# A one-core transformer block: one input loaded and split earlier, value products by unit, attention's matmuls moved between the rounded and the low blocks, turns of rows moved to later steps

## The chip, the cores and the metric

One core of a Trainium2 chip runs the whole kernel. The metric is the device time of one execution in microseconds (us). Engines: PE (TensorE) multiplies matrices, DVE (VectorE) and ACT (ScalarE) work on elements, POOL (GpSimd) does a few small things, SP (SyncE) issues most transfers; ACT's queue issues some too.

## The reference

One encoder layer on 256 tokens of width 2048, float32. Cut to what matters:

```
h = rms_norm(x, attn_norm);  proj = h @ w_in
qa, ka, va, qb, kb, vb, ga, gb = split(proj)
ya = windowed_gqa(qa, ka, va, table, sink)          # 8 heads, 2 key heads, |i-j| <= 128
yb = dilated_attention(qb, kb, vb, table)           # 3 groups of 4 heads, strides 1, 4, 16, merged per position
merged = sigmoid(ga) * (ya @ w_branch_a) + sigmoid(gb) * (yb @ w_branch_b)
x = x + merged @ w_out
hf = rms_norm(x, ffn_norm)
g = depthwise_conv3(hf @ w_ffn_gate)
x = x + (gelu(g) * (hf @ w_ffn_up)) @ w_ffn_down    # width 5632
x = x + sigmoid(rms_norm(x, ple_norm) @ w_ple_gate) * (p @ w_ple_proj)   # p: 256 x 256
return rms_norm(x, final_norm)
```

## The kernel before

Every weight is read once, in 263 pieces, mostly of 1 MB, that SP's queue loads into a ring of three buffers `raw` (L243). A piece is cut into units. For each unit ACT writes a rounded copy (L263, `uh` or `vh`) and DVE the remainder (L264, `ul` or `vl`), so that a float32 product is made of three products of the rounded type: rounded x rounded, rounded x low, low x rounded. Units of plain pieces live in a ring of six (`u`), those of Strassen pieces that need sums of weight blocks in a ring of two (`v`); the sums are three instructions on DVE, L256 to L258, ahead of the split. A unit is produced when the one that it replaces in its ring is dropped after its last matmul.

Stages, in order: A (the projections of queries, keys and values, with the attention heads in between), B0 to B3 with ba/bb (gates and branch products), D0 and D1 (output projection), E0 and E1 (gate and up), F00, F01, F10, F11 (down product, half of the inputs by half of the outputs each), pp0 and pp1 (p times `w_ple_proj`), G0, G2, G3 (the per-layer gate), then the final rows.

In A and E a job is one output block of 128 columns. It takes two units of eight blocks each (`unit_blocks`): sixteen matmuls of 128x512 with the rounded weights (L305; the 512 columns are the tokens' rounded and low halves), then sixteen of 128x256 with the low weights (L309). The value jobs are different (`value_product`): for each of sixteen blocks k, three matmuls into each of two banks (L343 to L345).

B, D, F, G0 and pp go by `quad_stage`: a piece of kind "S" is a Strassen step of 21 matmuls, one of kind "s" has 24 (L355 to L357). All are 128x512.

Small work hangs on steps. `at((stage, i, g), f)` registers f, and `run_due` calls it when the stage's loop arrives there. A head's scores are registered one job on at k = 9, the transposition of its softmax (`turn`, L666) in the job after that at k = 11 or 12, and its values (L612 to L614, and L681 for the far heads) another job on at k = 4. `turn` also copies the transposed rows to `near` on ACT and DVE, which the values need. `residual` adds the sums of D and F to the residual rows `xr` (L915, L917, and the square for the norm in L919), and `rows_pair` turns two blocks of 256 columns of these rows back (`turn_back`: four transpositions into one bank, L849, then two ACT L452 and two DVE L453 that write `pl`, the input of G). A bank such as P22 is one of eight in which matmuls add up; the sums M2, M3, M4, P22 of a stage keep theirs from their first matmul until L915 has read them.

The calls only give a dependence order and a program order as written; a scheduler then orders the instructions of each engine by its own cost estimates, except where `keep` fixes it.

The input p (`pair`, 256 KB) is needed in pp0 and pp1. Its rounded part is `ph_` (tiles `t`, L1001), its low part `pl_` (tiles `u`, L1002).

Of the kernel before, what the change touches and what calls it, by code (L numbers as in the profile page):

```python
# [187 lines left out]
def _encoder(ctx: ExitStack, tc, xt, pt, xrow, cols, gainrow, table, onehot, mask, ident_in, wts, out):  # L188
# [108 lines left out]
    def unit_blocks(todo):  # L297

        ends, units = [], []
        for _ in range(JOINED):  # L300
            u = _FBLOCKS[state["at"] + len(ends)][0]
            units.append(u)
            for o in range(_LAST_OF[u] + 1):
                acc, m, first, last = next(todo)
                nc.tensor.matmul(acc, weights(u)[0][:, o * P:(o + 1) * P], m,  # L305
                                 start=first, stop=False, skip_group_check=True)
                ends.append((acc, m, last, u, o))
        for acc, m, last, u, o in ends:
# [4 lines left out]
        state["at"] += len(ends)  # L313

    def products(i, moving, n, accs):

        def todo():
            for k in range(n):
                run_due(i, k)
                for acc in accs:  # L320
                    yield acc, moving(k), k == 0, k == n - 1

        blocks, end = todo(), state["at"] + n * len(accs)
        while state["at"] < end:
            unit_blocks(blocks)
# [7 lines left out]
    def value_product(i, paired, n):  # L333

        accs = [bank("acc") for _ in range(2)]
        for k in range(KC):
            run_due(i, k)
            u, o = _FBLOCKS[state["at"]]
            hi, lo = (w[:, o * P:(o + n) * P] for w in weights(u))
            for t, acc in enumerate(accs):  # L340
                tokens = (TWINS if paired else HALVES)[t]
                xh, xl = (hs[:, k, c:c + T][:, tokens] for c in (0, T))
                nc.tensor.matmul(acc[:, :n * P], xh, hi, start=(k == 0), stop=False)  # L343
                nc.tensor.matmul(acc[:, :n * P], xh, lo, start=False, stop=False)  # L344
                nc.tensor.matmul(acc[:, :n * P], xl, hi, start=False, stop=(k == KC - 1))  # L345
            state["at"] += n
            if o + n - 1 == _LAST_OF[u]:
                drop(u)
# [631 lines left out]

    for half in range(2):
# [14 lines left out]
        if half:  # L996
            pr = held["tok"].tile([P, 2, T], F32, name="pair", bufs=2)
            nc.scalar.dma_start(pr, pt)
            ph_, pl_ = ([sc.tile([P, T], FR, name=name) for _ in range(2)] for name in ("t", "u"))
            for k in range(2):  # L1000
                nc.scalar.activation(ph_[k], pr[:, k], AF.Copy)  # L1001
                nc.vector.tensor_tensor(pl_[k], pr[:, k], ph_[k].bitcast(F32), op=ALU.subtract)  # L1002
            held["ssq"] = sc.tile([P, 2, 2], F32, name="ssq", bufs=1)
        residual("F%d0" % half, 0, activation_row, "act", half)
        if half:
            pl = big.tile([P, KC, 2 * T], FR, name="pl", tag="R0")
            for pair, when in enumerate((("F11", 0, 2), ("F11", 0, 5), ("F11", 1, 0), ("F11", 1, 3))):
# [64 lines left out]
    for t in range(2):  # L1072
# [13 lines left out]
        for n in range(4):  # L1086
            row = xr[:, t, cut[n]]
            if n % 2:
# [58 lines left out]
```

## Time and profile before

| | |
|---|---|
| median of 3 runs | 1463.11 us (1462.89 to 1464.44) |
| profiled execution | 1462.99 us, of which the span of the profile is 1461.2 |
| PE | busy 1446.7 us, 7488 matmuls |
| DVE | busy 1248.4 us, 1839 instructions |
| ACT | busy 824.8 us, 1151 instructions |
| PE's granted clock | 0.998 of full speed |
| transferred | 282.88 MB, mean 194 GB/s |

The span is the time from the first to the last record on the core; the rest of the execution lies around it. A matmul's duration in the profile overlaps that of the next one, so the time between two starts is what a matmul takes of the run.

### The profile page before, as it was taken

Reading aid. Unit: us, or ns where it says so; the run is one execution under the profiler, and the core shown is the slowest. Engines: PE = TensorE matmul, PEld = TensorE weight load, DVE = VectorE, ACT = ScalarE, POOL = GpSimd, SP = SyncE. Lnnn points to the kernel's source line nnn. Section 1 sums busy time; section 2 is a strip of 40 time slices with the busy share of each in tenths; the row PEclk is TensorE's granted clock in tenths of the full one; section 3 lists DMA queues with packets and bytes.
Section 4 is the critical chain, followed back from the end, with each engine's and each line's share of the span. In section 5 each row is a group of like instructions: output and inputs, shape, how many; then the busy total and the mean of one; then the engine's idle time right before and its main releaser. Section 6 shows DMA issues by size and latency. Waiting matters only on the chain.

```text
span 1461.2 us, 19529 instructions
## 1 busy us (share of the span) xinstructions
PE 1446.7 (99%) x7488; PEld 1235.3 (85%) x7488; DVE 1248.4 (85%) x1839; ACT 824.8 (56%) x1151; POOL 4.9 (0%) x9
## 2 busy tenths in 40 slices
PE   9999999999999999999999999999999999999997
PEld 8888888888888888788888888888888888788785
DVE  7777664679998989989888899989888888999994
ACT  7555544456555655655555556555555555555763
POOL 0000000000000000000000000000000000000000
PEclk9999999999999999999999999999999999999999
DMA  9753444435546456465555545565455554546462
GB/s 323 259 206 144 169 160 166 174 138 202 199 187 238 180 205 233 170 247 185 192 184 193 183 172 200 200 232 202 181 194 185 190 189 164 192 183 235 168 231 86
DMA packets 46456, 282.88 MB, mean 194 GB/s; under 512 B 5076, under 2 KB 9812, under 8 KB 14108
## 3 DMA queue, kind: packets, MB, share of 16 engines
q1 hardware_dynamic: 45356, 280.20, 52.3%
q10 hardware_dynamic: 1008, 1.45, 0.3%
q8 instruction: 58, 0.95, 0.2%
q14 instruction: 34, 0.28, 0.1%
HBM read 279.49 MB, written 2.14 MB: 193 GB/s over the span
## 4 chain that ended last, share of the span: by engine, by line
PE 94%; DVE 2%; DMA 1%; ACT 1%; issue 1%; POOLq 0%; POOL 0%; ACTq 0%
PE bank L305 29%; PE bank L309 15%; PE bank L356 13%; PE bank L355 13%; PE bank L357 13%; PE bank L343 2%; PE bank L345 2%; PE bank L344 2%; PE bank L291 2%; PE bank L292 1%; DVE ul L264 1%; PE bank L849 1%; PE bank L666 0%; DMA pair<-in_pt 0%; DMA raw<-in_wts 0%
## 5 line engine op out<-in xcount | busy, mean ns | idle before, releaser
L263 ACT ACTIVATE uh<-raw 128x1024 fp32r<-128x1024 f32 (+2 forms) x518 | 521.8, 1017 | 397.9 <-PE bank L305 190.3
L264 DVE TENSOR_TENSOR ul<-raw,uh 128x1024 fp32r<-128x1024 f32 (+2 forms) x518 | 595.8, 1168 | 152.6 <-ACT uh L263 72.0
L305 PE MATMUL bank<-hf,uh 128*128 128x512 f32 x1408 | 336.5, 391 | 0.0
L305 PEld LDWEIGHTS bank<-hf,uh 128*128 128x128 f32 x1408 | 258.6, 188 | 50.1
L309 PEld LDWEIGHTS bank<-hf,ul 128*128 128x128 f32 x1408 | 180.6, 191 | 6.9
L309 PE MATMUL bank<-hf,ul 128*128 128x256 f32 x1408 | 183.0, 283 | 0.0
L263 ACT ACTIVATE vh<-raw 128x1024 fp32r<-128x1024 f32 x92 | 97.5, 1059 | 66.9 <-DVE raw L256 36.7
L264 DVE TENSOR_TENSOR vl<-raw,vh 128x1024 fp32r<-128x1024 f32 x92 | 111.8, 1217 | 0.4
L305 PE MATMUL bank<-hs,uh 128*128 128x512 f32 x432 | 109.2, 395 | 0.0
L355 PE MATMUL bank<-uh,act 128*128 128x512 f32 x232 | 90.4, 390 | 0.0
L357 PE MATMUL bank<-uh,act 128*128 128x512 f32 x232 | 90.4, 390 | 0.0
L356 PE MATMUL bank<-ul,act 128*128 128x512 f32 x232 | 90.4, 390 | 0.0
L305 PEld LDWEIGHTS bank<-hs,uh 128*128 128x128 f32 x432 | 77.7, 189 | 13.8
L436 ACT ACTIVATE t<-bank 128x256 f32<-128x256 f32 x122 | 46.4, 383 | 75.5 <-PE bank L309 70.1
L355 PE MATMUL bank<-uh,hs 128*128 128x512 f32 x172 | 67.3, 391 | 0.0
L357 PE MATMUL bank<-uh,hs 128*128 128x512 f32 x172 | 67.2, 391 | 0.0
L356 PE MATMUL bank<-ul,hs 128*128 128x512 f32 x172 | 67.1, 390 | 0.0
L309 PEld LDWEIGHTS bank<-hs,ul 128*128 128x128 f32 x432 | 55.4, 191 | 2.2
L256 DVE TENSOR_TENSOR raw<-raw 128x1024 f32<-128x1024 f32 x46 | 56.1, 1219 | 0.6
L356 PE MATMUL bank<-vl,S 128*128 128x512 f32 x138 | 54.4, 394 | 1.8 <-DVE vl L264 1.7
L309 PE MATMUL bank<-hs,ul 128*128 128x256 f32 x432 | 56.0, 282 | 0.0
L355 PE MATMUL bank<-vh,S 128*128 128x512 f32 x138 | 54.5, 399 | 0.3 <-ACT vh L263 0.3
(240 smaller groups left out, 2272.3 us busy)
## 6 DMA issues: line engine op xcount, KB each, us to landing
raw<-in_wts SPq DMA_DIRECT2D x251, 1024.0 KB, 4.8
raw<-in_wts SPq DMA_DIRECT2D x12, 512.0 KB, 6.7
xr<-in_xrow SPq DMA_DIRECT2D x4, 512.0 KB, 8.3
x<-in_xt SPq DMA_DIRECT2D x13, 128.0 KB, 5.7
hb<-hold SPq DMA_DIRECT2D x3, 514.0 KB, 5.9
hb<-hold SPq DMA_DIRECT2D x2, 768.0 KB, 7.1
last<-in_gainrow SPq DMA_DIRECT2D x1, 1024.0 KB, 5.0
out<-xr SPq DMA_DIRECT2D x4, 256.0 KB, 2.6
```

The lines of the kernel that those rows point to most:

```text
L256: nc.vector.tensor_tensor(raw[:, :2 * WIDE], raw[:, WIDE:3 * WIDE], raw[:, :2 * WIDE], op=ALU.subtract)
L263: nc.scalar.activation(hi, src, AF.Copy)
L264: nc.vector.tensor_tensor(lo, src, hi.bitcast(F32), op=ALU.subtract)
L291: nc.tensor.matmul(acc, hi[:, w], m, start=first, stop=False, skip_group_check=True)
L305: nc.tensor.matmul(acc, weights(u)[0][:, o * P:(o + 1) * P], m, start=first, stop=False, skip_group_check=True)
L309: nc.tensor.matmul(acc[:, T:], weights(u)[1][:, o * P:(o + 1) * P], m[:, :T], start=False, stop=last, skip_group_check=True)
L343: nc.tensor.matmul(acc[:, :n * P], xh, hi, start=(k == 0), stop=False)
L344: nc.tensor.matmul(acc[:, :n * P], xh, lo, start=False, stop=False)
L355: nc.tensor.matmul(acc, sh, wh, start=first, stop=False)
L356: nc.tensor.matmul(acc, sh, wl, start=False, stop=False)
L357: nc.tensor.matmul(acc, sl, wh, start=False, stop=last)
L436: keep(nc.scalar.activation(t, acc[:, T:], AF.Copy, scale=scale))
```

## The change

Five parts:
- `value_product` goes by unit: all blocks of a unit into the first bank, then all into the second (before: block by block, into both banks). What is due at k is run ahead of the first bank's matmuls of k.
- `unit_blocks` runs what is due at k up to 10 (scores, values) after the sixteen rounded matmuls and ahead of the sixteen low ones, and what is due at 11 to 13 (the transpositions) after the low ones. What is due at the first k of the two units still comes first. Before, all of it stood among the rounded matmuls.
- p is loaded by SP's queue at step (F10, 2, 0) and split at (F10, 9, 0). Before, it was loaded by ACT's queue and split in front of F10.
- In F11, the four turns of rows are registered at the steps (0, 6), (1, 2), (1, 5), (2, 1) instead of (0, 2), (0, 5), (1, 0), (1, 3).
- Of the final rows' four column blocks, DVE scales three and ACT one, instead of two each.

Line numbers move: L305 is L307 after, L309 L314, L343 to L345 L353 to L355, L355 to L357 L364 to L366, L447 and L448 L456 and L457, L612 to L614 L621 to L623, L666 L675, L681 L690, L849 L858, L974 and L975 L983 and L984, L1001 and L1002 L1000 and L1001.

PE's order in stage A, around one far head's values (`bank_1930` is the job's sum; `near` and `far` are the head's transposed rows). Before:

```order
L305 MATMUL bank_1930<-hs_102,uh_1766 128x512 x4
L612 MATMUL bank_1935<-near_1879,v_1109 128x256
L613 MATMUL bank_1935<-near_1879,v_1109 128x256
L614 MATMUL bank_1935<-near_1879,v_1109 128x256
L612 MATMUL bank_1935<-near_1879,v_1109 128x256
L613 MATMUL bank_1935<-near_1879,v_1109 128x256
L614 MATMUL bank_1935<-near_1879,v_1109 128x256
L681 MATMUL bank_1935<-far_1880,vf_1567 128x128 x4
L305 MATMUL bank_1930<-hs_102,uh_1766 128x512 x4
L305 MATMUL bank_1930<-hs_102,uh_1778 128x512 x8
L309 MATMUL bank_1930<-hs_102,ul_1767 128x256 x8
L309 MATMUL bank_1930<-hs_102,ul_1779 128x256 x8
```

The same job after, with the transpositions that end the job ahead of it:

```order
L675 MATMUL bank_1911<-ident_76,s_1805 128x128 x4
L675 MATMUL bank_1918<-ident_76,s_1805 128x128 x4
L307 MATMUL bank_1930<-hs_102,uh_1766 128x512 x8
L307 MATMUL bank_1930<-hs_102,uh_1778 128x512 x8
L621 MATMUL bank_1947<-near_1909,v_1109 128x256
L622 MATMUL bank_1947<-near_1909,v_1109 128x256
L623 MATMUL bank_1947<-near_1909,v_1109 128x256
L621 MATMUL bank_1947<-near_1909,v_1109 128x256
L622 MATMUL bank_1947<-near_1909,v_1109 128x256
L623 MATMUL bank_1947<-near_1909,v_1109 128x256
L690 MATMUL bank_1947<-far_1910,vf_1567 128x128 x4
L314 MATMUL bank_1930<-hs_102,ul_1767 128x256 x8
```

The sixteen 128x512 matmuls are one run, and the head's narrow ones stand against the low block.

DVE's order at the end of E1 and the start of F10 (`raw_11217` is the piece of the first Strassen units vl, `pair_11302` the last rows of the up product). Before:

```order
L440 TENSOR_TENSOR pair_11302<-bank_11310,t_11353 128x256
L1002 TENSOR_TENSOR u_11364<-pair_11360,t_11362 128x256
L974 SCALAR_TENSOR_TENSOR pair_11302<-pair_11302,rms_5783 128x256
L1002 TENSOR_TENSOR u_11365<-pair_11360,t_11363 128x256
L975 TENSOR_TENSOR pair_11302<-pair_11302,gw_11128 128x256
L256 TENSOR_TENSOR raw_11217<-raw_11217 128x1024
L264 TENSOR_TENSOR ul_11413<-raw_11284,uh_11412 128x1024
L448 TENSOR_TENSOR act2_8954<-pair_11302,act2_8954 128x256
L257 TENSOR_TENSOR raw_11217<-raw_11217 128x512
L264 TENSOR_TENSOR vl_11387<-raw_11217,vh_11386 128x1024
```

After:

```order
L449 TENSOR_TENSOR pair_11302<-bank_11310,t_11353 128x256
L256 TENSOR_TENSOR raw_11217<-raw_11217 128x1024
L983 SCALAR_TENSOR_TENSOR pair_11302<-pair_11302,rms_5813 128x256
L257 TENSOR_TENSOR raw_11217<-raw_11217 128x512
L984 TENSOR_TENSOR pair_11302<-pair_11302,gw_11128 128x256
L258 TENSOR_TENSOR raw_11217<-raw_11217 128x512
L264 TENSOR_TENSOR ul_11403<-raw_11284,uh_11402 128x1024
L457 TENSOR_TENSOR act2_8954<-pair_11302,act2_8954 128x256
L264 TENSOR_TENSOR vl_11377<-raw_11217,vh_11376 128x1024
```

The two subtractions for p are gone from here; they stand some twenty rows further down DVE's order, between two weight splits, and their partners on ACT (L1000) likewise.

PE's order in pp0 (`t` and `u` are the parts of p; `bank_12319`, `bank_12333`, `bank_12345` and `bank_12359` take pairs 4 to 7 of the rows, the last of these on P22). Before:

```order
L355 MATMUL bank_12355<-uh_12201,t_11363 128x512
L849 MATMUL bank_12359<-ident_76,xr_4920 128x128
L356 MATMUL bank_12355<-ul_12202,t_11363 128x512
L357 MATMUL bank_12355<-uh_12201,u_11365 128x512
L355 MATMUL bank_12390<-uh_12234,t_11362 128x512
L356 MATMUL bank_12390<-ul_12235,t_11362 128x512
L357 MATMUL bank_12390<-uh_12234,u_11364 128x512
```

After (`bank_11923` is pair 3's, on P22):

```order
L364 MATMUL bank_12355<-uh_12201,t_11721 128x512
L858 MATMUL bank_11923<-ident_76,xr_4920 128x128 x4
L365 MATMUL bank_12355<-ul_12202,t_11721 128x512
L366 MATMUL bank_12355<-uh_12201,u_11722 128x512
L364 MATMUL bank_12390<-uh_12234,t_11717 128x512
L365 MATMUL bank_12390<-ul_12235,t_11717 128x512
L366 MATMUL bank_12390<-uh_12234,u_11718 128x512
```

Pair 3, which stood in F11, has taken pair 7's place in pp0; pair 7 follows three products later. The first transposition of pair 0 stands 18 matmuls into F11 in both kernels.

```diff
--- before.py
+++ after.py
@@ -294,35 +294,41 @@
         if o == _LAST_OF[u]:
             drop(u)
 
-    def unit_blocks(todo):
-
-        ends, units = [], []
+    def unit_blocks(i, todo):
+
+        ends, ks = [], []
         for _ in range(JOINED):
             u = _FBLOCKS[state["at"] + len(ends)][0]
-            units.append(u)
             for o in range(_LAST_OF[u] + 1):
-                acc, m, first, last = next(todo)
+                acc, k, m, first, last = next(todo)
+                if not ks:
+                    run_due(i, k)
+                ks.append(k)
                 nc.tensor.matmul(acc, weights(u)[0][:, o * P:(o + 1) * P], m,
                                  start=first, stop=False, skip_group_check=True)
                 ends.append((acc, m, last, u, o))
+        early = [k for k in ks if k % KC <= 10]
+        for k in early:
+            run_due(i, k)
         for acc, m, last, u, o in ends:
             nc.tensor.matmul(acc[:, T:], weights(u)[1][:, o * P:(o + 1) * P], m[:, :T],
                              start=False, stop=last, skip_group_check=True)
             if o == _LAST_OF[u]:
                 drop(u)
         state["at"] += len(ends)
+        for k in ks:
+            run_due(i, k)
 
     def products(i, moving, n, accs):
 
         def todo():
             for k in range(n):
-                run_due(i, k)
                 for acc in accs:
-                    yield acc, moving(k), k == 0, k == n - 1
+                    yield acc, k, moving(k), k == 0, k == n - 1
 
         blocks, end = todo(), state["at"] + n * len(accs)
         while state["at"] < end:
-            unit_blocks(blocks)
+            unit_blocks(i, blocks)
         assert next(blocks, None) is None
 
     def product(i, moving, n, ring):
@@ -333,19 +339,22 @@
     def value_product(i, paired, n):
 
         accs = [bank("acc") for _ in range(2)]
-        for k in range(KC):
-            run_due(i, k)
+        per = SUB // n
+        for k0 in range(0, KC, per):
             u, o = _FBLOCKS[state["at"]]
-            hi, lo = (w[:, o * P:(o + n) * P] for w in weights(u))
+            assert o == 0 and _LAST_OF[u] == SUB - 1
             for t, acc in enumerate(accs):
                 tokens = (TWINS if paired else HALVES)[t]
-                xh, xl = (hs[:, k, c:c + T][:, tokens] for c in (0, T))
-                nc.tensor.matmul(acc[:, :n * P], xh, hi, start=(k == 0), stop=False)
-                nc.tensor.matmul(acc[:, :n * P], xh, lo, start=False, stop=False)
-                nc.tensor.matmul(acc[:, :n * P], xl, hi, start=False, stop=(k == KC - 1))
-            state["at"] += n
-            if o + n - 1 == _LAST_OF[u]:
-                drop(u)
+                for k in range(k0, k0 + per):
+                    if t == 0:
+                        run_due(i, k)
+                    hi, lo = (w[:, (k - k0) * n * P:(k - k0 + 1) * n * P] for w in weights(u))
+                    xh, xl = (hs[:, k, c:c + T][:, tokens] for c in (0, T))
+                    nc.tensor.matmul(acc[:, :n * P], xh, hi, start=(k == 0), stop=False)
+                    nc.tensor.matmul(acc[:, :n * P], xh, lo, start=False, stop=False)
+                    nc.tensor.matmul(acc[:, :n * P], xl, hi, start=False, stop=(k == KC - 1))
+            state["at"] += SUB
+            drop(u)
         return accs
 
 
@@ -978,6 +987,19 @@
             if n % 2 and DOWN[pair] == "S":
                 combos["act", pair] = sums_of(held["pair"], pair // 2)
 
+    ph_, pl_ = [], []
+
+    def load_last():
+        held["pr"] = held["tok"].tile([P, 2, T], F32, name="pair", bufs=2)
+        keep(nc.sync.dma_start(held["pr"], pt))
+
+    def split_last():
+        for k in range(2):
+            ph_.append(sc.tile([P, T], FR, name="t"))
+            pl_.append(sc.tile([P, T], FR, name="u"))
+            nc.scalar.activation(ph_[k], held["pr"][:, k], AF.Copy)
+            nc.vector.tensor_tensor(pl_[k], held["pr"][:, k], ph_[k].bitcast(F32), op=ALU.subtract)
+
     for half in range(2):
         held["act"] = [big.tile([P, 16, 2 * T], FR, name="act", tag="R1"),
                        [big.tile([P, 2 * T], FR, name="act1", tag="yb%d" % i) for i in range(4)],
@@ -994,17 +1016,13 @@
         for kind, n in jobs[joint:]:
             mlp(kind, n, product(stage, lambda k: hf[:, k, :], KC, "e"))
         if half:
-            pr = held["tok"].tile([P, 2, T], F32, name="pair", bufs=2)
-            nc.scalar.dma_start(pr, pt)
-            ph_, pl_ = ([sc.tile([P, T], FR, name=name) for _ in range(2)] for name in ("t", "u"))
-            for k in range(2):
-                nc.scalar.activation(ph_[k], pr[:, k], AF.Copy)
-                nc.vector.tensor_tensor(pl_[k], pr[:, k], ph_[k].bitcast(F32), op=ALU.subtract)
+            at(("F10", 2, 0), load_last)
+            at(("F10", 9, 0), split_last)
             held["ssq"] = sc.tile([P, 2, 2], F32, name="ssq", bufs=1)
         residual("F%d0" % half, 0, activation_row, "act", half)
         if half:
             pl = big.tile([P, KC, 2 * T], FR, name="pl", tag="R0")
-            for pair, when in enumerate((("F11", 0, 2), ("F11", 0, 5), ("F11", 1, 0), ("F11", 1, 3))):
+            for pair, when in enumerate((("F11", 0, 6), ("F11", 1, 2), ("F11", 1, 5), ("F11", 2, 1))):
                 at(when, rows_pair, "P22", pair, pl, 2)
             at(("F11", 2, 4), combine, "pl", pl, 0, 0)
             at(("F11", 4, 4), combine, "pl", pl, 2, 1)
@@ -1085,7 +1103,7 @@
         nc.vector.tensor_tensor(xr[:, t, cut[3]], xr[:, t, cut[3]], gains[:, cut[3]], op=ALU.mult)
         for n in range(4):
             row = xr[:, t, cut[n]]
-            if n % 2:
+            if n == 1:
                 nc.scalar.activation(row, row, AF.Copy, scale=r)
             else:
                 nc.vector.tensor_scalar(row, row, r, None, op0=ALU.mult)
```

## The prediction

> **What bounds the kernel now.** I read the shares of busy time first, then the chain of work that ended last, then the timeline wherever TensorE's (PE's) matmuls stand further apart than their steady step. Engine shares and the chain by engine:
>
> ```profile
> PE 1446.7 (99%) x7488; PEld 1235.3 (85%) x7488; DVE 1248.4 (85%) x1839; ACT 824.8 (56%) x1151; POOL 4.9 (0%) x9
> PE 94%; DVE 2%; DMA 1%; ACT 1%; issue 1%; POOLq 0%; POOL 0%; ACTq 0%
> ```
>
> PE is busy 1446.7 of 1461.2 us. The change removes no matmul, so all it can win lies in the 14.5 us in which PE is not busy and in matmuls that start further apart than they need to. The longest detour of the chain from PE is a transfer at the start of the stage F10. The chain's piece, then the timeline of the queues and engines there, then nine PE matmuls in a row (columns: start, length, what, idle time before and its releaser):
>
> ```profile
> 1232.70 6.78 DMA pair<-in_pt
> ...
> 1239.56 0.72 ACT L1001 ACTIVATE t<-pair 128x256 fp32r<-128x256 f32 x2 [3.40 <-DMA pair<-in_pt]
> 1240.01 0.43 DVE L1002 TENSOR_TENSOR u<-pair,t 128x256 fp32r<-128x256 f32 x1 [3.40 <-ACT t L1001]
> ...
> 1244.52 0.39 PE L355 MATMUL bank<-vh,S 128*128 128x512 f32 x1
> 1245.84 0.50 PE L356 MATMUL bank<-vl,S 128*128 128x512 f32 x1 [0.94 <-DVE vl L264]
> 1246.18 0.40 PE L357 MATMUL bank<-vh,S 128*128 128x512 f32 x1
> 1246.42 0.40 PE L355 MATMUL bank<-vh,S 128*128 128x512 f32 x1
> 1246.66 0.40 PE L356 MATMUL bank<-vl,S 128*128 128x512 f32 x1
> 1246.89 0.40 PE L357 MATMUL bank<-vh,S 128*128 128x512 f32 x1
> 1247.60 0.51 PE L355 MATMUL bank<-vh,S 128*128 128x512 f32 x1 [0.31 <-ACT vh L263]
> 1248.86 0.50 PE L356 MATMUL bank<-vl,S 128*128 128x512 f32 x1 [0.75 <-DVE vl L264]
> 1249.19 0.40 PE L357 MATMUL bank<-vh,S 128*128 128x512 f32 x1
> ```
>
> ACT and DVE each stand idle for 3.40 us behind the per-layer input p. What is queued behind on them is the weights of the first Strassen pieces, and four to eight microseconds later PE waits three times for vh and vl. The other places that the change touches are the start of F11, the product pp0, the attention heads and the end; their rows stand with their terms.
>
> **The steady step.** Three runs of PE's matmuls in the attention stage give it:
>
> ```profile
> 183.77 1.09 PE L305 MATMUL bank<-hs,uh 128*128 128x512 f32 x4
> 184.70 0.28 PE L612 MATMUL bank<-near,v 128*128 128x256 f32 x1
> ...
> 186.22 3.01 PE L305 MATMUL bank<-hs,uh 128*128 128x512 f32 x12
> 189.07 2.08 PE L309 MATMUL bank<-hs,ul 128*128 128x256 f32 x16
> 190.98 3.82 PE L305 MATMUL bank<-hs,uh 128*128 128x512 f32 x16
> 194.63 2.08 PE L309 MATMUL bank<-hs,ul 128*128 128x256 f32 x16
> ```
>
> Start to start, 16 undisturbed 128x512 matmuls take 194.63 - 190.98 = 3.65 us (0.228 each) and 16 of 128x256 take 190.98 - 189.07 = 1.91 us (0.119).
>
> **Part 1: p is loaded and split inside F10.** From 1244.52 to 1249.19 are eight steps in 4.67 us; at 0.228 they need 1.82, so 2.85 us are lost. After, DVE goes on without the 3.40 us, and without the two subtractions of 0.43 each, which moved to step 9: some 4.25 us sooner. The first vl was ready about 1245.8 and is then ready about 1241.6 to 1242.4, where PE needs it at 1244.75; the second, ready about 1248.8, comes at 1243.5 to 1244.6, where PE would need it at about 1246.1 (six steps after 1244.75). So all three stalls go: -2.8. What is late next: the two ACT and two DVE instructions (0.72 and 0.85 us) do not vanish, they are done near 1257, ahead of the units of the next piece. DVE's lead over PE there is larger than now by 4.25 - 2.85 = 1.4 us, so after paying 0.85 it is still 0.55 to the good. The new DMA stands on SP's queue between two weight loads and issues in about a third of a microsecond; it waits for nothing in the order, and the weight load behind it is the one that is held up by that third. Ends: -2.9 if nothing is given back, 0 if the whole of it comes back at the next pieces; the row nearest is the idle time of 3.40, and I take -2.8.
>
> **Part 2: turns of rows in F11 begin later.** Rows of the three places in F11 where PE stands:
>
> ```profile
> 1297.87 0.33 PE L849 MATMUL bank<-ident,xr 128*128 128x128 f32 x1 [0.66 <-DVE xr L915]
> ...
> 1316.44 0.39 PE L356 MATMUL bank<-ul,S 128*128 128x512 f32 x1
> 1316.83 0.50 PE L355 MATMUL bank<-vh,S 128*128 128x512 f32 x1
> ...
> 1329.22 0.39 PE L356 MATMUL bank<-ul,act 128*128 128x512 f32 x1
> 1329.60 0.50 PE L356 MATMUL bank<-vl,S 128*128 128x512 f32 x1
> ```
>
> The first transposition waits for the last sum of F10. By the new order it still stands 18 matmuls into F11, as before: the step number says later, the scheduler puts it at the same place. I leave that 0.66 us (0 to -0.7). The other two stalls are steps of 0.39 and 0.38 instead of 0.23, and each is followed by one step of 0.33 to 0.34: 0.25 each. They come while ACT and DVE also read the turned rows out (L452, L453) between weight splits. After, pair 3's read-out is gone from F11, so two instructions on each engine are off that queue: -0.5 (0 to -0.5).
>
> What moves out lands in pp0. Pair 3 uses the bank P22, F11's fourth sum takes that bank before it, and so its four transpositions now stand among pp0's matmuls, with pair 7 (also P22) behind it. Rows there (ACT, then PE):
>
> ```profile
> 1361.76 1.05 ACT L919 ACTIVATE c<-xr 128x1024 f32<-128x1024 f32 x1
> 1362.80 1.56 ACT L452 ACTIVATE pl<-bank,cl 128x256 fp32r<-128x256 f32 x4
> 1364.23 0.61 ACT L1041 ACTIVATE last<-bank 128x512 f32<-128x512 f32 x1
> 1364.89 0.50 PE L355 MATMUL bank<-uh,t 128*128 128x512 f32 x1 [0.33 <-ACT last L1041]
> ```
>
> PE waits for L1041, which sits on ACT behind the read-outs of the turned rows, and they behind the square of the last sum of F11 (L919). The new order puts two more read-outs (0.36 to 0.46 each) ahead of pair 7's transpositions, and a chain pair 3, read-out, pair 7, read-out on one bank. By walking ACT's queue, L1041 ends about 0.4 us later against the PE matmul that wants its bank: the stall of some 0.5 us becomes some 0.9: +0.4. Ends: 0, if the read-outs fit in ACT's gaps, and +2, if all four of the added and moved read-outs (4 x 0.45) and the transpositions end up ahead of L1041. The four transpositions cost the same in either place.
>
> **Part 3: attention's matmuls between the rounded and the low blocks.** Before, a head's matmuls cut a run of 128x512 in two. In the job from 183.77 the cut run takes (184.70 - 183.77) + (189.07 - 186.22) = 3.78 us against 3.65, and the low block 1.91 as undisturbed: 0.13 lost to the cut. Read job by job the same way, the 17 cut jobs lose 0.03 to 0.07 and three of them 0.13; together 0.85 us. After, each run of 16 is whole and a head's 256-wide matmuls come next to the 256-wide low block, so I take -0.7 (0 to -0.9). On the page "TensorE: Matmul & The Clock Gate", section "Back-to-back issue gap", the Trainium skill gives the isolated gap of a warm matmul as N/2.4 + 2.5 ns, a function of its own width alone (215.8 ns for 512). By that rule the neighbours' widths cost nothing, the 0.85 us would not come back and the sum would end at 1460.0; the trace, with 0.237 us in the cut run of 12 and 0.228 in the whole one, speaks against it.
>
> The wait that could replace it: the values need the turned rows' copy (near). The transpositions end at about 180.85 and the values start at 184.70: 3.85 us. After, 16 whole matmuls, 3.65 us, stand between. The copy needs one ACT and one DVE instruction, 1.4 to 2.1 us with what is queued, so it stays hidden. Scores to transpositions gets longer, not shorter.
>
> **Part 4: value products by unit.** The same matmuls in another order of banks. Groups in the window 79.1 to 84.4 (near keys), then 229 to 250 (far keys, whose tokens are read with a stride), PE rows:
>
> ```profile
> L343 PE MATMUL bank<-uh,hs 128*128 128x512 f32 x8 | 3.1, 391 | 0.0
> ...
> L343 PE MATMUL bank<-uh,hs 128*128 128x512 f32 x31 | 12.2, 394 | 0.0
> ```
>
> Both alternate between two banks; only the strided ones are slower. So the stride and not the alternation is what the rows speak for, and I take 0. If it were the alternation, the 192 matmuls of the far keys would gain the 3 ns by which they are longer and as much again in their spacing: -1.2 at most.
>
> **Part 5: the end.** The last normalisation factor, then the rows:
>
> ```profile
> 1455.46 1.33 ACT L1089 ACTIVATE xr<-xr,r 128x512 f32<-128x512 f32 x2 [1.29 <-POOL r L1084]
> 1455.46 0.88 DVE L1091 TENSOR_SCALAR xr<-xr,r 128x512 f32<-128x512 f32 x2 [0.45 <-POOL r L1084]
> 1456.21 0.95 ACTq L1092 DMA_DIRECT2D out<-xr  x2
> ```
>
> ACT's second row ends at 1456.79, and its output transfer follows. DVE does two in 0.88, three in about 1.3 (1456.76). That is -0.05 (0 to -0.1).
>
> **The sum.** -2.8 - 0.5 + 0.4 - 0.7 + 0 - 0.05 = -3.65 on the profiled execution of 1462.99 us (span 1461.2 and 1.8 around it), which is 0.1 below the median of 1463.11. That is 1459.3; against the median, 1459.4. I give 1459.4.
>
> **The rivals.**
> - F10's gain is given back: DVE is 85% busy over the span, and what it did not do before F10 it does at 1257. For it: the two splits stay on DVE's queue. Against it: 3.40 us of pure idle time vanish, and PE gains less than that. It would leave -0.4 of the -2.8: 1461.8. It decides if a vl or ul of the pieces after 1257 is over 0.5 us later than I take it.
> - pp0 takes the larger price, +2 in place of +0.4: 1461.0. For it: L1041 is already late there. It decides if pair 7's read-out stands ahead of the L1041 whose bank PE wants next.
> - The first transposition in F11 is no longer waited for (DVE is earlier from F10 on): -0.7 more, 1458.7. Against it: DVE there is held by PE's own F10 sums.
> - The value products gain by alternating less: 1458.2.
> - The whole runs of part 3 gain nothing, if what the cut run loses is lost at the head's own matmuls and moves with them: 0 in place of -0.7, 1460.1. For it: each run of 128x512 still follows narrower matmuls. Against it: the 12 matmuls behind the cut are the ones that are spaced at 0.237. This is also how the Trainium skill's rule above comes out.
> - Slower: the values wait for near in each of the 12 heads' groups. The window is 3.65 us; a copy queued behind two weight splits on each of ACT (1.06 each) and DVE (1.22 each) would need about 2 x 1.06 + 2 x 1.22 + 1.3 = 5.9. That is 2.2 us in each of 12 places, 27, less the sum's 3.65: 1486. With one split on each (3.6) it is just hidden, so it decides from the second split on. Against it is the stage's row, with the window only 0.2 us larger there and PE busy throughout:
>
> ```profile
> 60.00:310.00 250.00, 250.00 (x1422) 218.95 (x1421) 168.16 (x260) 129.25 (x210) 0.00 (x0) 1.00 0.49 178
> ```
>
> **How the numbers follow.** Chances: the forecast 0.45, whole runs gain nothing 0.12, first F11 stall gone 0.10, value products 0.08, pp0 dear 0.12, F10 given back 0.08, slower 0.05. About 0.2%, 2.9 us, can be told from no change, so faster means below 1460.2: the forecast and the three beside it, less what the errors of their terms put above the bound, 0.68. Within 0.2%: pp0 dear, F10 given back and that rest, 0.27. The range from 1457.3 (the value products with the first F11 stall gone too, and small terms at their better ends) to 1462.0 (F10 given back) leaves out some 0.15. The forecast's own range is 1458.5 to 1460.3.
>
> **What would show it.** Right: no idle time behind in_pt on ACT and DVE near 1239, PE's steps at 0.23 through F10's first Strassen piece; steps under 0.3 near 1316 and 1329; a wait for L1041's successor in pp0 of 0.8 to 1.0; runs of 16 at 3.65 in every attention job. Wrong: a new wait for vl or ul after 1257, waits for near or s in the attention, or a pp0 wait over 1.5 us.

## The result and the profile after

The changed kernel takes 1458.48 us (median of 7 runs, 1458.31 to 1459.38) against 1463.04 in the runs beside it: -4.56 us, a ratio of 0.9969 with a 95% interval of 0.9957 to 0.9980. The forecast was 1459.4. The profiled execution's span went from 1461.2 to 1456.6 us.

Engine shares and chain by engine of the page after:

```profile
PE 1445.2 (99%) x7488; PEld 1237.1 (85%) x7488; DVE 1248.2 (86%) x1841; ACT 824.1 (57%) x1149; POOL 4.9 (0%) x9
PE 98%; ACT 1%; issue 0%; DMA 0%; DVE 0%; POOLq 0%; POOL 0%; ACTq 0%; DVEq 0%
```

The chain that ended last is now 98% PE where it was 94%; the DMA's 1% and DVE's 2% have left it. The start of F10 in the timeline after, DVE first, then PE:

```profile
1239.33 1.22 DVE L264 TENSOR_TENSOR ul<-raw,uh 128x1024 fp32r<-128x1024 f32 x1
1240.47 0.42 DVE L457 TENSOR_TENSOR act<-pair,act 128x256 fp32r<-128x256 f32 x1
1240.80 2.35 DVE L264 TENSOR_TENSOR vl<-raw,vh 128x1024 fp32r<-128x1024 f32 x2
...
1244.31 0.39 PE L364 MATMUL bank<-vh,S 128*128 128x512 f32 x1
1244.54 0.39 PE L365 MATMUL bank<-vl,S 128*128 128x512 f32 x1
...
1245.90 0.39 PE L365 MATMUL bank<-vl,S 128*128 128x512 f32 x1
```

Both vl are ready by 1243.15, before PE's first use of the first at 1244.54; from 1244.31 to 1245.90 are seven steps in 1.59 us, 0.227 each. p itself lands 8.1 us after its issue on SP's queue, and ACT idles 0.60 us for it without a stall of PE (ACT):

```profile
1252.79 0.72 ACT L1000 ACTIVATE t<-pair 128x256 fp32r<-128x256 f32 x2 [0.60 <-DMA pair<-in_pt]
```

The first transposition of F11 (the DVE addition that it needs, then PE):

```profile
1293.24 0.68 DVE L924 TENSOR_TENSOR xr<-xr,bank 128x512 f32<-128x512 f32 x1
1293.97 0.33 PE L858 MATMUL bank<-ident,xr 128*128 128x128 f32 x1
```

The profile shows no idle time before it any more (0.66 us before). In pp0 (ACT, then PE):

```profile
1357.59 1.57 ACT L461 ACTIVATE pl<-bank,cl 128x256 fp32r<-128x256 f32 x4
1359.02 1.09 ACT L263 ACTIVATE uh<-raw 128x1024 fp32r<-128x1024 f32 x1
1359.97 0.63 ACT L1059 ACTIVATE last<-bank 128x512 f32<-128x512 f32 x1
...
1359.63 0.39 PE L366 MATMUL bank<-uh,u 128*128 128x512 f32 x1
1360.65 0.50 PE L364 MATMUL bank<-uh,t 128*128 128x512 f32 x1 [0.63 <-ACT last L1059]
```

That is the wait that grew, from a step of 0.73 to one of 1.02. In the attention, the far head's turn and values:

```profile
183.82 3.89 PE L307 MATMUL bank<-hs,uh 128*128 128x512 f32 x16
187.55 0.28 PE L621 MATMUL bank<-near,v 128*128 128x256 f32 x1
...
189.07 2.16 PE L314 MATMUL bank<-hs,ul 128*128 128x256 f32 x16
191.06 3.82 PE L307 MATMUL bank<-hs,uh 128*128 128x512 f32 x16
```

The run of 16 is whole (3.73 us start to start, since eight transpositions stand ahead of it; 3.65 where none do), the head's 14 narrow matmuls take 1.52, the low block 1.99.

Start-to-start times of PE's matmuls give the account between the two profiled executions:

| place | forecast | measured |
|---|---|---|
| F10, p's load and split | -2.8 | -2.85 |
| F11, the two stalls near 1316 and 1329 | -0.5 | -0.53 |
| F11, the first transposition | 0 (a rival: -0.7) | -0.80 |
| pp0, the wait for L1041/L1059 with the slow step behind it | +0.4 | +0.29 |
| pp1, a stall near 1379 | not named | -0.18 |
| attention, jobs from 60 to 305 us | -0.7 | -0.61 |
| value products | 0 | 0 |
| the end, behind PE's last matmul | -0.05 | -0.12 |
| start, up to 60 us | not named | +0.33 |

The sum is -4.47; the spans differ by 4.55, and the rest lies in steps too small to place. The start is not the change's: its code is the same up to the value products. In the execution of before the alternating matmuls there run at 0.347 us a pair behind a stall of 0.3 us at 12.84, in that of after at 0.353. Both spacings occur below in kernels with the same start (0.347 in p_only and turns_only, 0.353 in values_only and attn_only; no_turns has such a stall and 0.353), so the change does not choose between them. What does is not shown.

### The profile page after: what moved, and what is told of

Same layout as the page of the kernel before. It is cut to its first block, busy times and chain, and to the rows that moved or that the text cites. A ratio compares the mean times of both kernels' runs of the same rounds, so it can differ in the third digit from the quotient of the medians.

```text
span 1456.6 us, 19524 instructions
## 1 busy us (share of the span) xinstructions
PE 1445.2 (99%) x7488; PEld 1237.1 (85%) x7488; DVE 1248.2 (86%) x1841; ACT 824.1 (57%) x1149; POOL 4.9 (0%) x9
## 4 chain that ended last, share of the span: by engine, by line
PE 98%; ACT 1%; issue 0%; DMA 0%; DVE 0%; POOLq 0%; POOL 0%; ACTq 0%; DVEq 0%
PE bank L307 29%; PE bank L314 15%; PE bank L364 14%; PE bank L365 14%; PE bank L366 14%; PE bank L291 2%; PE bank L353 2%; PE bank L355 2%; PE bank L354 2%; PE bank L292 1%; PE bank L858 1%; PE bank L675 0%; PE bank L623 0%; PE bank L622 0%; PE bank L621 0%
## 5 line engine op out<-in xcount | busy, mean ns | idle before, releaser
L307 PE MATMUL bank<-hf,uh 128*128 128x512 f32 x1408 | 336.4, 391 | 0.0
L307 PEld LDWEIGHTS bank<-hf,uh 128*128 128x128 f32 x1408 | 258.9, 188 | 50.2
L314 PEld LDWEIGHTS bank<-hf,ul 128*128 128x128 f32 x1408 | 180.4, 191 | 6.7
L314 PE MATMUL bank<-hf,ul 128*128 128x256 f32 x1408 | 182.8, 283 | 0.0
L307 PE MATMUL bank<-hs,uh 128*128 128x512 f32 x432 | 103.6, 392 | 0.0
L307 PEld LDWEIGHTS bank<-hs,uh 128*128 128x128 f32 x432 | 79.5, 188 | 15.6
L364 PE MATMUL bank<-uh,act 128*128 128x512 f32 x232 | 90.4, 390 | 0.0
L366 PE MATMUL bank<-uh,act 128*128 128x512 f32 x232 | 90.3, 389 | 0.0
L364 PE MATMUL bank<-uh,hs 128*128 128x512 f32 x172 | 67.3, 391 | 0.0
L366 PE MATMUL bank<-uh,hs 128*128 128x512 f32 x172 | 67.2, 391 | 0.0
L314 PE MATMUL bank<-hs,ul 128*128 128x256 f32 x432 | 56.6, 284 | 0.0
L314 PEld LDWEIGHTS bank<-hs,ul 128*128 128x128 f32 x432 | 54.5, 191 | 1.0
L364 PE MATMUL bank<-vh,S 128*128 128x512 f32 x138 | 54.3, 398 | 0.0
```

The costliest lines, as they stand in the source:

```text
L314: nc.tensor.matmul(acc[:, T:], weights(u)[1][:, o * P:(o + 1) * P], m[:, :T], start=False, stop=last, skip_group_check=True)
L364: nc.tensor.matmul(acc, sh, wh, start=first, stop=False)
L366: nc.tensor.matmul(acc, sl, wh, start=False, stop=last)
```

## The experiments

Two theories at the outset, on the one large miss (the first wait of F11). L: DVE's lead from F10 carries through to it. T: the later steps of the turns take it away. The kernel before, run beside each of three groups, took 1463.10, 1463.15 and 1463.27 us.

**p_only**: only p's load and split from the diff, on the kernel before.

```diff
...
-            nc.scalar.dma_start(pr, pt)
...
+            at(("F10", 2, 0), load_last)
+            at(("F10", 9, 0), split_last)
```

> The kernel before with only the load and split of p moved into F10. Theory L (DVE's lead): without the 3.40 us of waiting, DVE runs ahead of PE by more than PE gains, and that lead is still there at the start of F11. So the three stalls of F10 go (-2.85) and with them the wait for the first transposition of F11 (-0.82): about 1459.4 us. Rival T (the turns' new steps took that wait away): -2.85 only, about 1460.2, and the first transposition still waits some 0.7 us for xr. Under both the two small stalls of F11 (0.25 each) may stay.

Measured: 1460.94 us, ratio 0.9984 (0.9975 to 0.9992). All stalls at F10's start are gone, but the first transposition of F11 waits as before, and pp0 has a wait at its fourth transposition, the first of pair 7 on the bank P22, that the profile of before does not show (PE rows):

```profile
1295.10 0.33 PE L849 MATMUL bank<-ident,xr 128*128 128x128 f32 x1 [0.58 <-DVE xr L915]
...
1356.24 0.33 PE L849 MATMUL bank<-ident,xr 128*128 128x128 f32 x1 [0.55 <-DVE xr L915]
```

So L is wrong, and part of F10's 2.85 is given back in pp0: the median gains 2.2 us, less than either theory said.

**turns_only**: only the steps of the turns.

```diff
-            for pair, when in enumerate((("F11", 0, 2), ("F11", 0, 5), ("F11", 1, 0), ("F11", 1, 3))):
+            for pair, when in enumerate((("F11", 0, 6), ("F11", 1, 2), ("F11", 1, 5), ("F11", 2, 1))):
```

> The kernel before with only the later turns of rows in F11. Theory L: the first transposition still waits 0.7 to 0.8 us; the two small stalls (0.5 together) go; the wait in pp0 grows from 0.5 to 0.8: net -0.2, about 1462.8 us. Rival T: the first wait goes too, -1.0 in all, about 1462.0.

Measured: 1462.73 us, ratio 0.9996 (0.9987 to 1.0005). The two stalls near 1316 and 1329 are gone; the first wait is still there, so T is wrong too:

```profile
1297.95 0.33 PE L849 MATMUL bank<-ident,xr 128*128 128x128 f32 x1 [0.45 <-DVE xr L915]
```

**attn_only**: only `unit_blocks` and its caller.

```diff
...
+        early = [k for k in ks if k % KC <= 10]
+        for k in early:
+            run_due(i, k)
...
```

> The kernel before with only unit_blocks changed, so that attention's matmuls stand between the rounded and the low blocks. Theory W (whole runs of 128x512 save what the cuts cost): the stage from its first two-unit job to its end is 0.6 us shorter than before, about 1462.4 us. Rival N (the cuts' cost moves with the narrow matmuls): no change, 1463.0.

Measured: 1462.36 us, ratio 0.9993 (0.9985 to 1.0002): the interval does not tell it from no change, but the profile does. The stage from its first two-unit job to its end takes 244.29 us start to start against 244.91, as W says. In all the profiles of this document it takes 244.90 to 244.91 in the six kernels without this part and 244.25 to 244.30 in the eight with it. That the median is where W put it is partly luck: in the two profiles a slower start (+0.74) and a longer wait in pp0 (+0.3) hide a gain that W did not name. For here, where F10's stalls are all still there, the first wait of F11 is gone (ACT waiting for a weight load in F10, then PE at F11; the kernel before's ACT row ahead of them):

```profile
1281.39 1.58 ACT L263 ACTIVATE uh<-raw 128x512 fp32r<-128x512 f32 x2 [2.04 <-DMA raw<-in_wts]
```

```profile
1280.44 0.63 ACT L263 ACTIVATE uh<-raw 128x512 fp32r<-128x512 f32 x1 [0.91 <-DMA raw<-in_wts]
...
1297.23 0.29 PE L855 MATMUL bank<-ident,xr 128*128 128x128 f32 x1
```

The order of instructions on PE, DVE, ACT and SP from E1 to the end is the same in these two kernels. What differs is when one weight load lands: both issue it some 1275.2 us into the span, and it takes 6.1 us in one and 5.0 in the other. ACT's split is late by that, DVE's behind it, and in the kernel before DVE has no idle time from there to F11 to make it up: the last row of F10 comes late to the transposition.

**values_only**: only `value_product`.

```diff
...
-        for k in range(KC):
...
+        for k0 in range(0, KC, per):
...
             for t, acc in enumerate(accs):
...
+                for k in range(k0, k0 + per):
...
```

> The kernel before with only the value products by unit. Theory S (the spacing comes from the strided tokens, not from alternating banks): the last value job's 96 matmuls take 22.4 us as before, no change, 1463.0 us. Rival A (alternating): 96 x 6 ns less there, 21.8 us, and some -1.2 in all, 1461.8.

Measured: 1463.34 us, ratio 0.9998 (0.9989 to 1.0006). The last value job's 96 matmuls take 22.39 us start to start in the kernels before and after alike. PE rows of this run for that job:

```profile
L347 PE MATMUL bank<-uh,hs 128*128 128x512 f32 x32 | 12.6, 394 | 0.0
L348 PE MATMUL bank<-ul,hs 128*128 128x512 f32 x31 | 12.2, 394 | 0.0
```

394 ns as before: the order of the banks is worth nothing, and A is out. That the tokens' stride makes the difference, as S says, rests on the comparison of the near with the far keys alone; no run changed the stride.

**no_turns**: the changed kernel with the old steps of the turns.

```diff
-            for pair, when in enumerate((("F11", 0, 6), ("F11", 1, 2), ("F11", 1, 5), ("F11", 2, 1))):
+            for pair, when in enumerate((("F11", 0, 2), ("F11", 0, 5), ("F11", 1, 0), ("F11", 1, 3))):
```

> The changed kernel with the turns of rows in F11 put back to their old steps. Theory D (the first wait of F11 hangs on when one weight load lands, some 16 us earlier: in the profiles so far 5.0 to 5.3 us from issue to landing where the wait is gone, 5.9 to 6.1 where it is 0.6 to 0.8): the turns' steps have no part in that wait; what comes back is two stalls of 0.25 in F11 and 0.2 in pp1, less what pp0 wins: about 1459.2 us. Rival T (the later steps take it away together with the lead of F10): the wait comes back too, about 1460.0.

Measured: 1459.26 us, so by the medians the turns are worth some 0.8 us in the changed kernel (the ranges overlap). The load lands after 5.39 us and the first wait is down to 0.07: as D says. The two stalls of F11 are back, and so is a wait for xr at pp0's fourth transposition, which the later turns had taken away as well:

```profile
1313.08 0.50 PE L364 MATMUL bank<-vh,S 128*128 128x512 f32 x1
...
1325.86 0.50 PE L365 MATMUL bank<-vl,S 128*128 128x512 f32 x1
...
1354.94 0.33 PE L858 MATMUL bank<-ident,xr 128*128 128x128 f32 x1 [0.23 <-DVE xr L924]
```

**pair3_pp1**: the changed kernel, pair 3's turn in pp1.

```diff
-            for pair, when in enumerate((("F11", 0, 6), ("F11", 1, 2), ("F11", 1, 5), ("F11", 2, 1))):
+            for pair, when in enumerate((("F11", 0, 6), ("F11", 1, 2), ("F11", 1, 5))):
...
+    at(("pp1", 0, 5), rows_pair, "P22", 3, pl, 2)
```

> The changed kernel with pair 3 turned in pp1 (step 0, 5) instead of pp0. If the wait in pp0 (0.9 with its slow second step) comes from pair 3 and pair 7 sharing a bank and from two more read-outs on ACT ahead of L1060, it shrinks to 0.4 to 0.6: 1458.1 us. Rival: it comes from the four read-outs of pairs 4 to 7 that stand ahead of that L1060 in any case, so pp0 waits some 0.8 as before, and pp1 may wait in addition: 1458.5 to 1459.

Measured: 1457.93 us (1457.86 to 1458.53). The wait in pp0, with the slow step behind it, falls from 0.90 to 0.61, and pp1 gets none:

```profile
1359.74 0.50 PE L364 MATMUL bank<-uh,t 128*128 128x512 f32 x1 [0.34 <-ACT last L1060]
```

So pair 3's two read-outs did cost about 0.3 there; the other 0.61 comes from what is left.

**late_first**: as pair3_pp1, the first transposition nine matmuls later (the edit against pair3_pp1).

```diff
-            for pair, when in enumerate((("F11", 0, 6), ("F11", 1, 2), ("F11", 1, 5))):
+            for pair, when in enumerate((("F11", 1, 2), ("F11", 1, 3), ("F11", 1, 5))):
```

> As pair3_pp1, and the first transposition of F11 stands 27 matmuls into the stage instead of 18 (turns at the steps 1,2 / 1,3 / 1,5). Theory D: nine matmuls are 2 us, more than the 0.8 that the row is late when the load is slow, so no execution has the wait: as pair3_pp1 where that has a fast load, and a narrower spread of times. If the wait were of another kind (the bank, the engine's queue), it would come again behind the 27th matmul.

Measured: 1458.26 us (1457.99 to 1458.77), within the spread of pair3_pp1. There is no wait at the transposition, though the load took 5.54 us here, but the times are not tighter. It adds little: by the table below a load of 5.54 us would have cost an estimated 0.2 us at the old place.

**split_twice**: the changed kernel, p split twice.

```diff
+        for k in range(2):
+            nc.scalar.activation(ph_[k], held["pr"][:, k], AF.Copy)
+            nc.vector.tensor_tensor(pl_[k], held["pr"][:, k], ph_[k].bitcast(F32), op=ALU.subtract)
```

> The changed kernel with p's split done twice at its new place (two more instructions on ACT, 0.72 us, and two on DVE, 0.85). It measures the lead that is left on DVE there, which I took to be 0.55 us. If that holds, PE stalls by about 0.3 us more at the pieces behind 1257: 1458.8 us. If the lead is larger than 0.85, nothing changes: 1458.5. If DVE is the bound from there to F11, the whole 0.85 shows, at the first transposition of F11: 1459.3.

Measured: 1458.37 us, no new wait of PE anywhere in F10 or F11. The lead left on DVE at the split is over 0.85 us, not 0.55.

That left the question why that load lands late without the attention part. In every profile one 16,384-byte packet of the queue q8 starts near it. I take these for PE's instructions: there are 58 such packets in the page of before (`q8 instruction: 58, 0.95, 0.2%`), against 14,976 matmuls and weight loads of PE, and 59 in that of fetch_earlier below, whose profile has 24 instructions of PE more. The Trainium skill's page "Runtime: NRT & Kernel Launch", section "Instruction fetch mechanics", says that instructions are refilled in 16 KiB blocks of 256 over a DMA queue of the engine's own, and calls the cost mostly hidden; 58 x 256 = 14,848 fits the count. Theory I: the packet holds one of the 16 DMA engines for 0.93 us, and the load, which ends with its slowest engine, is late when the packet falls among its own.

**fetch_earlier**: the kernel before, with more and shorter warm-up matmuls, so that PE's packets come earlier.

```diff
-    for _ in range(WARM):
+    for _ in range(WARM - 6):
         nc.tensor.matmul(idle, ones, ones, start=True, stop=True)
+    for _ in range(12):
+        nc.tensor.matmul(idle[:, :P // 2], ones, ones[:, :P // 2], start=True, stop=True)
```

> The kernel before; of PE's 14 warm-up matmuls ahead of the first real one, six are replaced by twelve of half the width, so that every later PE instruction stands some 24 places further along in PE's stream and its blocks of instructions are fetched 2 to 3 us earlier against the work. Theory I (the weight load issued at 1275 lands late because PE's 16 KB instruction packet, 0.93 us on one of the DMA engines, starts 1.6 to 3.2 us after it is issued; where the packet starts by 1.1 us, it lands by 5.5): the packet comes ahead of the load's own packets, the load lands in 4.8 to 5.4 us instead of 6.1, the first transposition of F11 no longer waits, about 1462.3 us. Rival V (something else in the attention part decides): it lands at 5.9 to 6.1 and the wait of 0.6 to 0.8 stays, 1463.1.

Measured: 1462.56 us, ratio 0.9998 (0.9989 to 1.0007), so the times do not settle it; the profile does. The DMA view of before, in the 5.1 us from 1276.2 in which the load runs, then at its issue:

```profile
q8 instruction: 1, 0.02, 1.1%
...
raw<-in_wts SPq DMA_DIRECT2D x1, 1024.0 KB, 6.1
```

Here, in the 2.2 us ahead of the issue, then at the issue, then PE at F11:

```profile
q8 instruction: 1, 0.02, 2.6%
...
raw<-in_wts SPq DMA_DIRECT2D x1, 1024.0 KB, 4.7
...
1296.17 0.28 PE L851 MATMUL bank<-ident,xr 128*128 128x128 f32 x1
```

With the packet 1.5 us ahead of the load, it lands after 4.75 us and the wait is gone, with nothing changed but the warm-up. (In this execution p's load landed after 5.77 us instead of 6.78, and the first of F10's three stalls, 1.1 us, is missing with it, so its 1461.16 is not the typical time.)

**fetch_later**: the changed kernel, with fewer and longer warm-up matmuls.

```diff
...
-    for _ in range(WARM):
-        nc.tensor.matmul(idle, ones, ones, start=True, stop=True)
+    for _ in range(WARM - 12):
+        nc.tensor.matmul(idle[:, :P], ones, ones, start=True, stop=True)
+    for _ in range(6):      # moving operand of twice the width
...
```

> The changed kernel; twelve of the warm-up matmuls are replaced by six of twice the width, so that PE's instruction packets come 2 to 3 us later against the work. Theory I: the packet near that load starts some 3 us after it is issued instead of 0.65, the load lands at 5.9 to 6.1 us instead of 5.3, and the wait for the first transposition of F11 is there, 0.4 to 0.8: about 1459.1 us. Rival V: nothing changes, 1458.5.

Measured: 1459.04 us, but not for the expected reason. The packet moved further than I reckoned, to 6.48 us after the issue, when the load (5.25 us) had landed; F11's first transposition does not wait. The profile has 0.47 us of waiting at 944, for a vl that the other profiles have in time, and 0.27 at pp0's fourth transposition. So this run agrees with I and does not test it.

**no_attn**: the changed kernel with the old `unit_blocks`.

```diff
...
-        early = [k for k in ks if k % KC <= 10]
-        for k in early:
-            run_due(i, k)
...
```

> The changed kernel with unit_blocks as before. The attention part's own 0.6 us come back in stage A; and by what the other runs showed so far, the first wait of F11 comes with it (0.6 to 0.8), since every profile without that part has it: about 1459.8 us. If the wait is absent here, the two are not tied, and it is 1459.1.

Measured: 1460.03 us, 1.5 above the changed kernel. The packet starts 1.11 us after the issue and lasts 1.36, the load lands after 5.84, and the wait is back (0.52 start to start):

```profile
1295.29 0.33 PE L852 MATMUL bank<-ident,xr 128*128 128x128 f32 x1 [0.36 <-DVE xr L918]
```

**pairs37_pp1**: as pair3_pp1, with pair 7 moved too (the edit against pair3_pp1).

```diff
-    for pair, which in enumerate(("M2", "M3", "M4", "P22")):
+    for pair, which in enumerate(("M2", "M3", "M4")):
         at(("pp0", 0, 4 + pair), rows_pair, which, 4 + pair, pl, 2)
...
+    at(("pp1", 0, 7), rows_pair, "M2", 7, pl, 2)
```

> The changed kernel with pair 3 turned in pp1 as in pair3_pp1, and pair 7 too (bank M2). In pp0 only pairs 4 to 6 are left, so one read-out on ACT less stands ahead of the L1060 that PE waits for (0.35 to 0.45 us each). The wait of 0.5 in pp0 falls to 0.1 or less, if pp1 has room for four read-outs: 1457.5 us. If ACT or DVE is late in pp1 instead (it had 0.2 to 0.4 of waits there in some runs), nothing is won: 1457.9 to 1458.3.

Measured: 1457.56 us (1456.95 to 1458.56), ratio 0.9960 (0.9948 to 0.9973): the fastest median of all, 0.9 below the changed kernel, though the ranges overlap (1458.31 to 1458.56). pp0's wait and its slow step are 0.29, pp1 has none. In the profile the instruction packet stood 1.29 us after the load's issue, which then took 5.68, and 0.36 of the first wait of F11 is back:

```profile
1293.97 0.33 PE L858 MATMUL bank<-ident,xr 128*128 128x128 f32 x1 [0.20 <-DVE xr L924]
...
1359.61 0.50 PE L364 MATMUL bank<-uh,t 128*128 128x512 f32 x1
```

The load, the packet and the wait in all the profiles (us; the packet is counted from the load's issue; the wait is the step into the transposition less a steady step of 0.23):

| kernel | packet starts | packet ends | load lands after | first wait of F11 |
|---|---|---|---|---|
| before | 1.78 | 2.69 | 6.14 | 0.82 |
| p_only | 1.73 | 2.67 | 6.06 | 0.74 |
| values_only | 3.19 | 4.12 | 5.98 | 0.66 |
| turns_only | 1.60 | 2.54 | 5.93 | 0.61 |
| no_attn | 1.11 | 2.46 | 5.84 | 0.52 |
| pairs37_pp1 | 1.29 | 2.28 | 5.68 | 0.36 |
| late_first | 0.74 | 2.15 | 5.54 | none (stands later) |
| no_turns | 1.07 | 2.00 | 5.39 | 0.07 |
| pair3_pp1 | 0.71 | 2.05 | 5.37 | 0.06 |
| after | 0.65 | 1.95 | 5.34 | 0.02 |
| fetch_later | 6.48 | 7.45 | 5.25 | none |
| split_twice | 0.83 | 1.76 | 5.17 | none |
| attn_only | 0.67 | 1.61 | 5.01 | none |
| fetch_earlier | -1.49 | -0.56 | 4.75 | none |

Two regularities stand in it. Every wait is the landing less 5.32 us, to 0.01. And in the eleven profiles in which the packet starts 0.65 to 1.78 us after the issue, the load lands 3.31 to 3.44 us after the packet's end. The end counts and not the start: no_turns and no_attn start it at 1.07 and 1.11, but it lasts 0.93 us in the one and 1.36 in the other, and the load lands 0.45 later.

The packets in the traces show why one small packet is enough. Each of these loads comes with sixteen 4-byte packets, by my reading one at the end of each DMA engine's share. In the profile of before fifteen of them start 3.95 to 4.43 us after the issue and the sixteenth at 5.66. In fetch_earlier, with the packet out of the way, all sixteen start at 3.95 to 4.39. So one share alone is late, and the load is complete only with it. In six profiles that cost PE 0.36 to 0.82 us at F11.

## Why the prediction was right or wrong

- **p in F10: right.** All three stalls went, 2.85 against 2.8, and nothing came back at 1257. The lead that I took for 0.55 us is larger (split_twice). But p_only, alone, gained 2.2 us: without the other parts pp0 waits more (steps that add to 1.1 instead of 0.6).
- **Turns: the terms in F11 and pp0 right in kind and size** (-0.53 for -0.5, +0.29 for +0.4). What I missed is that with fewer read-outs in F11, the last rows are also earlier for pp0's fourth transposition: the last sum is added 4.9 to 5.0 us after pp0's start in seven of the eight profiles with later turns (5.6 in fetch_later, with a wait of 0.27), and 5.1 to 6.1 in the six with the old steps. In four of the five profiles with the old steps and without the shifted warm-up PE waits there or at L1041 for 0.8 to 1.1 in all, and the profile of before, with 0.6, was the lucky one. By no_turns the part is worth 0.8, by turns_only 0.4, not the 0.1 of my sum.
- **The first wait of F11: the step that failed.** I left it in place, with its disappearance as a rival at 0.10 for the reason that "DVE is earlier from F10 on". The size of the rival (-0.7) was right, the reason was not: p_only has that earlier DVE and the wait, attn_only has neither. It hangs on a weight load that landed after 5.8 to 6.1 us in five kernels without the attention part (4.75 in the sixth, with the shifted warm-up) and after 5.0 to 5.7 with it. I had read the load's time off the one profile as if it belonged to the work; it belongs to what else moves at that moment.
- **Attention: right in size, 0.61 for 0.7, in part by errors that cancel.** I read 0.85 us lost to the cuts; start to start the 18 cut jobs of before lose 1.82 in their rounded blocks, and 0.56 of it remains after. So the rounded blocks gain 1.25, not 0.7, and the transpositions 0.27 (0.89 us for a far head's eight before, 0.79 after). But the low blocks, which I took to stay at 1.91, lose 0.58 (1.99 behind a far head's 128-wide matmuls), the value jobs, of which more now start behind transpositions, 0.27, and the heads' own matmuls 0.07. The rival that the cost moves with the narrow matmuls was thus about half right.

  The sign that I named, runs of 16 at 3.65 in every job, holds in 20 of 27; the seven behind transpositions take 3.73 to 3.76. The 0.237 that I held against the rule of spacing was a mean: the first step of that run is 0.31, the others 0.22 to 0.24. By the isolated gap on the Trainium skill's page "TensorE: Matmul & The Clock Gate", section "Back-to-back issue gap", which goes by the matmul's own width, nothing would have been gained; the trace disagrees, since a run behind eight transpositions takes 3.73 us against 3.65 at the same width. The values did not wait for near in any profile.
- **Value products: right, 0. The end: right in kind, with 0.12 for 0.05.**
- **The total** is 0.9 us below the forecast, nearly all of it the first wait of F11: what came is the rival that I gave 0.10, and 1458.48 lies at the lower edge of the forecast's own range. That the rest of the sum is good to 0.1 is partly luck: the start's +0.33 and pp1's -0.18 were not in it, and p's part (2.2 alone) and the turns (0.4 to 0.8) are worth other amounts outside this sum.

That the first wait goes with the landing, and the landing with the end of the instruction packet, is shown by the 14 profiles and by the one run that moved the packet alone. That the attention part removes the wait by moving this packet follows from them, but it is no property of the part: pairs37_pp1 has the part and 0.36 of the wait. Open are why the packet lasts 0.92 us in some profiles and up to 1.41 in others, and how much its place differs between executions, since each kernel has one profile. The run meant to bring the wait back missed its place.

## What to carry to other kernels

An engine that stands idle behind a small late transfer can cost more than the transfer's size suggests: here 256 KB on ACT's queue cost 2.85 us of PE five to nine microseconds later in the profile, and splitting it inside F10, where DVE had a lead of over 0.85 us, cost PE nothing. Before pricing a stall of under a microsecond, ask for two or three sister profiles: which of the small waits appears changes from one nearly identical kernel to the next, and a part measured alone and the same part taken out of the whole differed by 0.4 to 0.8 us here. Work that shares one bank or one engine's queue with a product (the read-outs in pp0) should go to the next stage if its result is not needed before: of pp0's 0.90, 0.29 went with pair 3 and 0.32 more with pair 7.

## What the runs showed of the hardware that I had not expected

A refill of PE's instructions, one 16 KB packet of 0.92 to 1.41 us, made the 1 MB load near 1275 that it runs into land 3.31 to 3.44 us after the packet's end: after 5.0 to 6.1 us in eleven profiles where it starts 0.65 to 1.78 us after the load's issue (5.98 in a twelfth, where it starts at 3.19), against 4.75 and 5.25 where it comes before the load or after the landing. So a few PE instructions more or less in an early stage can add or remove a wait much later: 24 more at the start of fetch_earlier took away 0.82 us at 1297. And after a narrow matmul the next wide one starts late: the run of 16 behind transpositions takes 0.08 us more than behind a low block, of whichever job.
